# Nineteen slots for the experts' weights, a float32 gather one pair ahead, a down projection in column halves, and padded addresses

## The chip, the cores and the metric

The kernel runs on one core of a Trainium2 chip. A core has a matrix engine (TensorE, PE in the profile, with its weight loads as PEld), VectorE (DVE), ScalarE (ACT), GpSimd (POOL) and SyncE (SP), which here issues the transfers, and 16 DMA engines. The metric is the device time of one execution in microseconds; lower is better. The kernel before takes 2124.92 us, the median of three runs (2123.91 to 2125.03 us).

## The reference

Two transformer blocks over 256 tokens of 1024 features, in float32. The first is a hybrid layer: sparse attention, a gated recurrence and retention, merged through branch and output projections, and then a hierarchical mixture of experts. The second has four feed-forward layers, a spatial gating unit and stick-breaking attention. The change lies around the experts:

```python
gates = (jax.nn.one_hot(g_sel, N_GROUPS, dtype=jnp.float32)[:, :, None] * w_group[:, None, :]).astype(x.dtype)
...
for gi in range(N_GROUPS):
    hg = jax.nn.silu(jnp.einsum('nd,edf->nef', x, wg[gi])) * jnp.einsum('nd,edf->nef', x, wu[gi])
    y = y + jnp.einsum('nef,efd->nd', hg * gates[:, gi, :, None], wd[gi])
```

There are 4 groups of 8 experts, of width 512; a token takes one group and two of its experts, so that most of the gates are zero.

## The kernel before

Almost all matmuls outside the experts work on weights that come in units of 1 MB. `stage` (L214) loads a unit into one of three `ws` buffers. `load_split` rounds half of it to float32r on ScalarE (`wh`, L247) and subtracts on VectorE (`wl`, L248), and `mm3` (L268 to L270) multiplies weights and data, each in two parts, in three float32r matmuls. `wh` and `wl` have rings of three buffers in the pool `stg`; in the second block a further pool, `whx`, gives three more of each (`whx`, `wlx`), and the two rings are used in turn, three and three.

The experts (`experts`, L1121) go by pairs, 16 of them. A pair takes 12 units of 1 MB: for each of its two experts two for gate, two for up and two for down, 192 units in all. They lie in 13 slots: seven `b8` buffers (`we`), three `wx`, three `ws`. `route` fills all slots ahead (L1182). `both` consumes two slots, one for each expert of the pair, whose outputs stand in the two halves of the partitions, and then issues two further loads, which SyncE starts when the slot's last reader is done. A float32 matmul shows as two records in the profile, so a call of `both` is 16 records.

Up to 64 tokens (`CAP`) of an expert are gathered by a matmul with one-hot places. `places` makes them on VectorE for four experts at once (128x512). `gather` multiplies the normalized rows, in two float32r parts `hi` and `lo`, with the places, 256 columns for a chunk `k` of 128 features; each `k` has a PSUM bank of its own, and ScalarE copies it out with gain and shift (L1158, 128x256). A quad of experts is gathered one quad ahead, in halves, one in each pair.

`pair` (L1198) runs gate and up (four calls of `both`), silu on ScalarE (L1208), the product on VectorE (L1209), the previous pair's `spread`, four transposes of the product (L1214) with their copy (`actT`, L1216), the transposes of the places (L1221), the gates (L1223), `gsl` on VectorE (L1227), `ot` on ScalarE (L1228), the gather ahead (L1156), down (two calls of `both`, each over half of the inputs and all 1024 columns in two banks), and `dh` (L1237) and `dl` (L1238), the result in two float32r parts. `spread` (L1246, L1247) adds them to the tokens' rows with eight matmuls. After pair 0, a branch (`overflow`) handles experts with more than 64 tokens, and is not taken with these inputs.

The order on each engine is set when the program is built, by a scheduler with simulated times (`schedule_with_timeline_sim=True`), except where a chain or a `no_sync` fixes it.

Of the kernel before, what the change touches and what calls it, by code (L numbers as in the profile page):

```python
# [34 lines left out]
NE_B8, NE_MIX = 7, 3  # L35
ADA_EVERY, ADA_FROM = 3, 6
FRONT = 4
TCK = dict(schedule_with_timeline_sim=True)
# [80 lines left out]
def pack(inp):  # L119
# [39 lines left out]
    ed = g("expert_w_down")[0].reshape(NE, 2, 2, 128, 1024).transpose(0, 1, 3, 2, 4).reshape(NE, 2, 128, 2048)  # L159
# [21 lines left out]
class Program:  # L181
# [45 lines left out]
    def load_split(self, ap, kt, n=2048):  # L227
# [227 lines left out]
    def run(self):  # L455
        tc, nc, d = self.tc, self.nc, self.d
        with ExitStack() as es:
            self.main = es.enter_context(tc.tile_pool(name="main", bufs=1))
            self.small = es.enter_context(tc.tile_pool(name="small", bufs=1))
            self.stg = es.enter_context(tc.tile_pool(name="stg", bufs=3))  # L460
# [17 lines left out]
            self.hi = main.tile([128, KT, S], F32R, name="hi")  # L478
            self.lo = main.tile([128, KT, S], F32R, name="lo")
# [3 lines left out]
            eights = ExitStack()  # L483
            self.b8p = eights.enter_context(tc.tile_pool(name="b8", bufs=1))
# [4 lines left out]
            eights.close()  # L489
            self.whx = es.enter_context(tc.tile_pool(name="whx", bufs=1))  # L490
            self.ffn(0, fg)
# [14 lines left out]
            self.last_norm(g)  # L506

# [146 lines left out]
    def ada_row(self, chunk, o):  # L654
# [4 lines left out]
        r = self.small.tile([KT, 128], F32, name="adar", bufs=1)  # L659
# [50 lines left out]
    def hybrid(self):  # L710
# [89 lines left out]
        ocs = self.retention(at, cv, oc)  # L800
        self.branch(36, ocs, 8, mg, False, nk=4)
# [319 lines left out]
    def experts(self):  # L1121
# [3 lines left out]
        km, C = self.km, self.cap_limit  # L1125
        iota = km[:, 192:320]
        with tc.tile_pool(name="exw", bufs=1) as exw:
            xgs = [self.b8([128, KT, 4, CAP], name="xg") for _ in range(2)]
            self.slots = ([self.b8([128, 2048], name="we") for _ in range(NE_B8)]
                          + [exw.tile([128, 2048], F32, name="wx", bufs=NE_MIX) for _ in range(NE_MIX)]  # L1130
                          + [self.stg.tile([128, 2048], F32, name="ws", bufs=WS) for _ in range(WS)])
            self.units = [(2 * p + j, u) for p in range(NE // 2) for u in range(6) for j in range(2)]
            self.nload = self.nuse = 0
            with tc.tile_pool(name="moer", bufs=1) as self.moer:
                rank, topi, gates = self.route(km)
            with tc.tile_pool(name="moew", bufs=1) as self.moew:
                yp = self.acc4()
                ohs = {}

                def places(q):  # L1140

                    e4 = slice(4 * q, 4 * q + 4)
                    ohs[q] = oh = self.moew.tile([128, 2, 4, CAP], F32R, name="oh", bufs=2)
                    V.tensor_tensor(oh, iota[:, None, None, :CAP].to_broadcast([128, 2, 4, CAP]),
                                    rank[:, :, e4, None].to_broadcast([128, 2, 4, CAP]), op=OP.is_equal)
                    if C < CAP:
                        V.memset(oh[..., C:].bitcast(F32), 0.0)

                def gather(q, ks):

                    oh, xg = ohs[q], xgs[q % 2]
                    parts = [(hz, t) for hz in (self.hl, self.hh) for t in range(2)]
                    for k in ks:
                        ps = self.mms()[:, :4 * CAP].rearrange("p (a c) -> p a c", a=4)
                        for i, (hz, t) in enumerate(parts):
                            nc.tensor.matmul(ps, hz[:, t, k * 128:k * 128 + 128], oh[:, t], start=(i == 0), stop=(i == 3))  # L1156
# [3 lines left out]
                places(0)  # L1160
                gate, rgs = gates()
                gather(0, range(KT))
                pend = None
                for p in range(NE // 2):
                    q, ks = p // 2 + 1, range(4 * (p % 2), 4 * (p % 2) + 4)

                    def ahead():
                        if 4 * q < NE:
                            if p % 2 == 0:
                                places(q)  # L1170
                            gather(q, ks)

                    pend = self.pair(p, xgs[p // 2 % 2], ohs[p // 2], gate, yp, pend, ahead)
                    if p == 0:
                        self.overflow(topi, rgs, iota)
                self.spread(*pend)
                self.residual(yp, self.gt2)

    def load_slot(self):

        if self.nload < len(self.units):
            self.nc.sync.dma_start(self.slots[self.nload % len(self.slots)], self.d["w_e"][self.units[self.nload]])  # L1182
            self.nload += 1

    def both(self, outs, xs, ks, w, order):


        ws = [self.slots[(self.nuse + j) % len(self.slots)] for j in range(2)]
# [9 lines left out]
    def pair(self, p, xg, oh, gate, yp, pend, ahead):  # L1198
        nc, moe, V = self.nc, self.moew, self.nc.vector
        j0, e0, order = 2 * p % 4, 2 * p, []  # L1200
        ps = []
        for z in range(2):
            ps.append(self.mms())
            for u in range(2):
                self.both([(ps[z], 0)], lambda k: [xg[:, k, j0 + j] for j in range(2)], range(4 * u, 4 * u + 4),
                          lambda w, k, c: w[:, k % 4 * 512:k % 4 * 512 + 512], (order, KT - 1))
        a = moe.tile([128, 512], F32, name="act")
# [7 lines left out]
        at = moe.tile([128, 4, 2, CAP], F32, name="actT")  # L1215
# [3 lines left out]
        o2 = [oh[:, t, j0:j0 + 2].rearrange("p a c -> p (a c)").bitcast(F32) for t in range(2)]  # L1219
# [4 lines left out]
        ot = moe.tile([128, S], F32R, name="ot", bufs=2)  # L1224
        gs = moe.tile([128, 1], F32, name="gsl", bufs=2)
# [23 lines left out]
    def route(self, km):  # L1249

        nc, d, moer, small = self.nc, self.d, self.moer, self.small
        V, edge = nc.vector, self.edge
        before, iota = km[:, :128], km[:, 192:320]
        for _ in self.slots:
# [6 lines left out]
        ones = moer.tile([128, 128], F32R, name="ones_r")  # L1261
        nc.gpsimd.tensor_copy(ones, self.ones)
        earlier = moer.tile([128, 128], F32R, name="before_r")
# [4 lines left out]
        junk = moer.tile([128, 512], F32, name="rjunk")  # L1268
        xT = moer.tile([128, 2, KT, 128], F32, name="xT")
        ss, rs, lg = sm(2, "ssr"), small.tile([128, 2], F32, name="rsr"), sm(36, "lg")  # L1270
        hh = self.hh = self.hi.rearrange("p (a k) t -> p a (k t)", a=2)
        hl = self.hl = self.lo.rearrange("p (a k) t -> p a (k t)", a=2)
# [40 lines left out]
        self.chain(edge[1], nc.scalar.activation(hh[:, 0], self.x[:, 0], AF.Copy, scale=rs[:, 0:1]))  # L1313
        self.chain(edge[0], V.scalar_tensor_tensor(hl[:, 0], self.x[:, 0], rs[:, 0:1], hh[:, 0].bitcast(F32), op0=OP.mult, op1=OP.subtract))
# [6 lines left out]
        self.chain(edge[1], nc.scalar.activation(hh[:, 1], self.x[:, 1], AF.Copy, scale=rs[:, 1:2]))  # L1321
# [23 lines left out]
        found = V.tensor_mul(sel.rearrange("p a (g e) -> p a g e", g=4), og4, ssel[:, :, None, :].to_broadcast([128, 2, 4, 8]))  # L1345
        self.no_sync(V.scalar_tensor_tensor(hl[:, 1], self.x[:, 1], rs[:, 1:2], hh[:, 1].bitcast(F32), op0=OP.mult, op1=OP.subtract), found)
# [38 lines left out]
    def overflow(self, topi, rgs, iota):  # L1385

        nc, d, tc, moe = self.nc, self.d, self.tc, self.moew
# [429 lines left out]
```

## Time and profile before

| What | Value |
|---|---|
| median of three runs | 2124.92 us (2123.91 to 2125.03) |
| the profiled execution | 2124.35 us |
| its span | 2122.5 us |
| TensorE busy | 2044.1 us, 96% of the span |
| VectorE busy | 1111.3 us, 52% |
| ScalarE busy | 842.3 us, 40% |
| mean granted clock of TensorE | 0.993 |
| transfers | 503.17 MB, mean 237 GB/s |

The time of an execution is its span and some time around it. A share of busy time is a mean over the whole program; the expert stage lies at about 641 to 1117 us, the second block behind it. TensorE's records overlap, so that a row's duration is longer than the distance to the next row. A name such as `mm<-wh,hi` gives the output and the two operands.

### The profile page before, as it was taken

Reading aid. Unit: us, or ns where it says so; the run is one execution under the profiler, and the core shown is the slowest. Engines: PE = TensorE matmul, PEld = TensorE weight load, DVE = VectorE, ACT = ScalarE, POOL = GpSimd, SP = SyncE. Lnnn points to the kernel's source line nnn. Section 1 sums busy time; section 2 is a strip of 40 time slices with the busy share of each in tenths; the row PEclk is TensorE's granted clock in tenths of the full one; section 3 lists DMA queues with packets and bytes.
Section 4 is the critical chain, followed back from the end, with each engine's and each line's share of the span. In section 5 each row is a group of like instructions: output and inputs, shape, how many; then the busy total and the mean of one; then the engine's idle time right before and its main releaser. Section 6 shows DMA issues by size and latency. Waiting matters only on the chain.

```text
span 2122.5 us, 29320 instructions
## 1 busy us (share of the span) xinstructions
PE 2044.1 (96%) x12228; PEld 1608.6 (76%) x12228; DVE 1111.3 (52%) x1596; ACT 842.3 (40%) x1200; POOL 26.9 (1%) x40
## 2 busy tenths in 40 slices
PE   7999999999997999989989999999999999999998
PEld 5889889777773444333338998878999999989997
DVE  5886876755551111000017556656555755685555
ACT  4454334344442111111116445545444644475443
POOL 0000000000000000000000000000000000000000
PEclk9999999999998999999999999999999999999999
DMA  8655546455476999999995555544555455434552
GB/s 330 233 192 205 180 157 219 169 220 186 166 300 256 422 421 421 421 421 421 421 400 194 193 187 210 209 153 166 181 196 183 176 178 185 173 120 147 191 184 94
DMA packets 72124, 503.17 MB, mean 237 GB/s; under 512 B 8218, under 2 KB 10034, under 8 KB 11698
## 3 DMA queue, kind: packets, MB, share of 16 engines
q1 hardware_dynamic: 71986, 501.24, 62.1%
q8 instruction: 98, 1.61, 0.3%
q14 instruction: 40, 0.33, 0.0%
HBM read 500.14 MB, written 1.07 MB: 236 GB/s over the span
## 4 chain that ended last, share of the span: by engine, by line
PE 52%; DMA 12%; DVE 2%; issue 1%; ACT 0%; POOLq 0%; DVEq 0%; POOL 0%; SPq 0%; ACTq 0%
PE mm L268 10%; PE mm L270 10%; PE mm L269 10%; DMA we<-in_w_e 7%; PE mm L1193 6%; PE bg L268 5%; PE bg L270 5%; PE bg L269 5%; DMA ws<-in_w_e 3%; DMA wx<-in_w_e 3%; PE mm L411 1%; PE mm L1156 1%; DVE wl L248 0%; ACT wh L247 0%; DVE sn L1740 0%
## 5 line engine op out<-in xcount | busy, mean ns | idle before, releaser
L248 DVE TENSOR_TENSOR wl<-ws,wh 128x1024 fp32r<-128x1024 f32 x341 | 415.2, 1221 | 340.0 <-ACT wh L247 339.0
L247 ACT CAST wh<-ws 128x1024 fp32r<-128x1024 f32 x341 | 356.0, 1047 | 476.1 <-PE mm L270 386.3
L268 PE MATMUL mm<-hi,wl 128*128 128x256 f32 x1112 | 314.7, 283 | 2.7 <-DVE wl L248 2.6
L269 PE MATMUL mm<-lo,wh 128*128 128x256 f32 x1112 | 312.7, 281 | 0.1
L270 PE MATMUL mm<-hi,wh 128*128 128x256 f32 x1112 | 311.9, 280 | 0.0
L248 DVE TENSOR_TENSOR wlx<-ws,whx 128x1024 fp32r<-128x1024 f32 x165 | 201.1, 1222 | 141.5 <-ACT whx L247 141.2
L247 ACT CAST whx<-ws 128x1024 fp32r<-128x1024 f32 x165 | 172.3, 1049 | 174.5 <-PE mm L270 98.8
L268 PEld LDWEIGHTS mm<-hi,wl 128*128 128x128 f32 x1112 | 209.4, 188 | 6.4 <-DVE wl L248 3.9
L269 PEld LDWEIGHTS mm<-lo,wh 128*128 128x128 f32 x1112 | 209.5, 188 | 2.1 <-DVE lo L602 0.7
L270 PEld LDWEIGHTS mm<-hi,wh 128*128 128x128 f32 x1112 | 209.4, 188 | 0.7 <-issue 0.6
L269 PE MATMUL mm<-wl,hi 128*128 128x512 f32 (+1 forms) x468 | 179.9, 385 | 0.0
L268 PE MATMUL mm<-hi,wlx 128*128 128x256 f32 x640 | 179.0, 280 | 0.5 <-ACT rrow L1535 0.5
L270 PE MATMUL mm<-hi,whx 128*128 128x256 f32 x640 | 178.9, 279 | 0.0
L269 PE MATMUL mm<-lo,whx 128*128 128x256 f32 x640 | 178.7, 279 | 0.0
L270 PE MATMUL mm<-wh,hi 128*128 128x512 f32 (+1 forms) x468 | 177.5, 380 | 0.0
L268 PE MATMUL mm<-wh,lo 128*128 128x512 f32 (+1 forms) x468 | 173.9, 387 | 1.1 <-DVE lo L425 1.1
L1193 PE MATMUL mm<-we,xg 128*64 128x512 f32 x608 | 161.4, 599 | 4.7 <-DMA we<-in_w_e 4.7
L1209 DVE TENSOR_TENSOR act<-act,mm 128x512 f32<-128x512 f32 x16 | 11.0, 687 | 270.7 <-PE mm L1193 270.7
L268 PEld LDWEIGHTS mm<-hi,wlx 128*128 128x128 f32 x640 | 120.4, 188 | 1.8 <-ACT rrow L1535 0.8
L1193 PEld LDWEIGHTS mm<-we,xg 128*64 128x64 f32 x608 | 50.0, 138 | 94.6 <-issue 83.2
L269 PEld LDWEIGHTS mm<-lo,whx 128*128 128x128 f32 x640 | 120.5, 188 | 0.7
L270 PEld LDWEIGHTS mm<-hi,whx 128*128 128x128 f32 x640 | 120.5, 188 | 0.0
(490 smaller groups left out, 3432.6 us busy)
## 6 DMA issues: line engine op xcount, KB each, us to landing
we<-in_w_e SPq DMA_DIRECT2D x105, 1024.0 KB, 19.8
ws<-in_w_fi SPq DMA_DIRECT2D x88, 1024.0 KB, 4.8
wx<-in_w_e SPq DMA_DIRECT2D x45, 1024.0 KB, 19.8
ws<-in_w_fo SPq DMA_DIRECT2D x44, 1024.0 KB, 4.7
ws<-in_w_e SPq DMA_DIRECT2D x42, 1024.0 KB, 19.8
ws<-in_w_a SPq DMA_DIRECT2D x40, 1024.0 KB, 4.8
ws<-in_w_b SPq DMA_DIRECT2D x26, 1024.0 KB, 4.7
adw<-in_ada SPq DMA_DIRECT2D x17, 1024.0 KB, 7.2
```

The source lines that it names most:

```text
L247: w1 = nc.scalar.copy(wh[:, :m], src)
L248: w2 = nc.vector.tensor_sub(wl[:, :m], src, wh[:, :m].bitcast(F32))
L268: first = mm(out, ll, rh, start=start, stop=False)
L269: mm(out, lh, rl, start=False, stop=False)
L270: self.last_mm = mm(out, lh, rh, start=False, stop=stop)
L411: ins = nc.tensor.transpose(pss[k % 2][:, (k // 2) * 128:(k // 2) * 128 + 128], self.x[:, t, k * 128:k * 128 + 128], self.ident)
L1156: nc.tensor.matmul(ps, hz[:, t, k * 128:k * 128 + 128], oh[:, t], start=(i == 0), stop=(i == 3))
L1193: ins = self.nc.tensor.matmul(ps[j * 64:j * 64 + 64], xs(k)[j], w(ws[j], k, c), start=(k == 0), stop=(k == order[1]))
L1209: V.tensor_mul(a, a, ps[1])
```

## The change

- The slots: 19 in place of 13. `wp`, a tile of a new pool `exs`; `wr`, the place of `lo`; eight `b8` buffers; four `wx`; three `ws`; and two `whl` buffers. For the last, `wh` and `wl` become one tile `whl` of two halves, with two buffers, and a third of its own (`whd`), which in the experts holds first `xT` and then `dh` and `dl`. The first slot's load is issued in the hybrid layer, behind the last matmul of retention.
- The gather: float32 rows `xn` in one part, so that `lo` and the two VectorE subtractions that make it (L1314, L1346) are gone. Per pair 16 float32 matmuls of 128 columns, places of 128x256 for a pair, always one pair ahead (in pairs 0 to 14; before in 0 to 13). Four chunks `k` share a PSUM bank, and each of them has its own copy on ScalarE (128x128), in program order between the chunks' matmuls.
- The down projection: the weights are packed so that a unit holds half of the columns for all inputs. One call of `both` makes one half, and its `dh` and `dl` come before the other half's matmuls in program order.
- The addresses: unused tiles of 320, 128, 128 and 224 bytes a partition (`PADS`) in the pools `small`, `exs`, `whx` and `sgu`, and a longer `sn` in stick-breaking attention, move what lies behind them. `dynamic_dma_scratch_size=1024` is given to the compiler.
- `gsl`, `adar`, `act`, `ot` and the buffers of `overflow` change places; `overflow` follows the new packing.

The core of the diff:

```diff
-NE_B8, NE_MIX = 7, 3
+NE_B8, NE_MIX, NSLOT = 8, 4, 19
+PADS = 320, 128, 128, 224
...
-    ed = g("expert_w_down")[0].reshape(NE, 2, 2, 128, 1024).transpose(0, 1, 3, 2, 4).reshape(NE, 2, 128, 2048)
+    ed = g("expert_w_down")[0].reshape(NE, 4, 128, 2, 512).transpose(0, 3, 2, 1, 4).reshape(NE, 2, 128, 2048)
...
+    def pad(self, pool, n, name):
+
+        pool.tile([128, n // 4], F32, name=name)
+
...
+    def whl(self, shape, dt, last):
+        return self.stg.tile(shape, dt, name="whd", bufs=1) if last else self.stg.tile(shape, dt, name="whl", bufs=WHL - 1)
+
...
-            j = self.nhalf % (WHL + WH2)
+            j = self.nhalf % (WHL + WH2 if self.whx else WHL)
...
-                wh = self.stg.tile([128, 1024], F32R, name="wh", bufs=WHL)
-                wl = self.stg.tile([128, 1024], F32R, name="wl", bufs=WHL)
+                whl = self.whl([128, 2, 1024], F32R, j == WHL - 1)
+                wh, wl = whl[:, 0], whl[:, 1]
...
+            self.pad(self.small, PADS[0], "pad0")
...
+            self.exs = eights.enter_context(tc.tile_pool(name="exs", bufs=1))
+            self.slots = [self.exs.tile([128, 2048], F32, name="wp")]
...
+            self.pad(self.exs, PADS[1], "pad1")
...
+            self.pad(self.whx, PADS[2], "pad2")
...
+        self.no_sync(self.load_slot(), self.last_mm)
         self.branch(36, ocs, 8, mg, False, nk=4)
...
+        self.xn, spare = [self.main.tile([128, 2, 1024], F32, name=n, tag="hl", bufs=2) for n in ("xnr", "wr")]
+        with tc.tile_pool(name="exw", bufs=1) as self.exw:
+            self.slots.append(spare.rearrange("p a c -> p (a c)"))
+            self.slots += [self.b8([128, 2048], name="we") for _ in range(NE_B8)]
+            xgs = self.b8([128, 2, KT, 2, CAP], name="xg")
+            self.slots += [self.exw.tile([128, 2048], F32, name="wx", bufs=NE_MIX) for _ in range(NE_MIX)]
+            self.slots += [self.stg.tile([128, 2048], F32, name="ws", bufs=WS) for _ in range(WS)]
+            self.slots += [self.whl([128, 2048], F32, False) for _ in range(WHL - 1)]
+            rank, topi, gates = self.route(km)
+            self.dhl = self.whl([128, 2, 2, 512], F32R, True)
...
+            def gather(p):
+
+                oh, xg = ohs[p], xgs[:, p % 2]
+                for k0 in range(0, KT, 4):
+                    ps = self.mms().rearrange("p (k a c) -> p k a c", k=4, a=2)
+                    for k in range(k0, k0 + 4):
+                        for t in range(2):
+                            nc.tensor.matmul(ps[:, k - k0], self.xn[:, t, k * 128:k * 128 + 128], oh[:, t], start=(t == 0), stop=(t == 1))
                         gain, shift = self.a2c[:, k:k + 1], self.sh2c[:, k:k + 1]
-                        nc.scalar.activation(xg[:, k], ps, AF.Identity, bias=shift, scale=gain)
...
+                        nc.scalar.activation(xg[:, k], ps[:, k - k0], AF.Identity, bias=shift, scale=gain)
...
+                if p + 1 < NE // 2:
+                    places(p + 1)
+                    gather(p + 1)
...
-        pd = self.mms(2)
-        for u in range(2):
-            self.both([(pd[h], h * 512) for h in range(2)], lambda k: [at[:, k, j] for j in range(2)], range(2 * u, 2 * u + 2),
-                      lambda w, k, c: w[:, k % 2 * 1024 + c:k % 2 * 1024 + c + 512], (order, 3))
-        dh = self.stg.tile([128, 2, 512], F32R, name="dh", tag="wh", bufs=WHL)
-        dl = self.stg.tile([128, 2, 512], F32R, name="dl", tag="wl", bufs=WHL)
+        dh, dl = self.dhl[:, 0], self.dhl[:, 1]
         for h in range(2):
-            nc.scalar.activation(dh[:, h], pd[h], AF.Copy, scale=gs)
-            V.scalar_tensor_tensor(dl[:, h], pd[h], gs, dh[:, h].bitcast(F32), op0=OP.mult, op1=OP.subtract)
+            pd = self.mms()
+            self.both([(pd, 0)], lambda k: [at[:, k, j] for j in range(2)], range(4),
+                      lambda w, k, c: w[:, k * 512:k * 512 + 512], (order, 3))
+            nc.scalar.activation(dh[:, h], pd, AF.Copy, scale=gs)
+            V.scalar_tensor_tensor(dl[:, h], pd, gs, dh[:, h].bitcast(F32), op0=OP.mult, op1=OP.subtract)
...
-        for _ in self.slots:
+        while self.nload < NSLOT:
             self.load_slot()
...
-        xT = moer.tile([128, 2, KT, 128], F32, name="xT")
+        xT = self.whl([128, 2, KT, 128], F32, True)
...
-        self.chain(edge[1], nc.scalar.activation(hh[:, 0], self.x[:, 0], AF.Copy, scale=rs[:, 0:1]))
-        self.chain(edge[0], V.scalar_tensor_tensor(hl[:, 0], self.x[:, 0], rs[:, 0:1], hh[:, 0].bitcast(F32), op0=OP.mult, op1=OP.subtract))
+        self.chain(edge[1], nc.scalar.activation(self.xn[:, 0], self.x[:, 0], AF.Copy, scale=rs[:, 0:1]))
...
+        self.pad(sp, PADS[3], "pad3")
...
-                sn = sp.tile([128, 4 * S + 8], F32, name="sn", bufs=2)
+                sn = sp.tile([128, 4 * S + 64], F32, name="sn", bufs=2)
```

## Rows read from the trace of the kernel before

**Rows 1.** Windows: stretch, length, engines' busy time, clock, DMA share, GB/s.

```profile
635.00:650.00 15.00, 10.19 (x56) 7.47 (x57) 6.38 (x33) 5.16 (x11) 1.01 (x2) 0.77 0.01 2
...
700.00:836.00 136.00, 132.60 (x642) 55.73 (x641) 13.84 (x27) 22.69 (x43) 0.00 (x0) 1.00 1.01 421
836.00:1096.00 260.00, 239.52 (x1129) 98.36 (x1127) 23.63 (x46) 40.44 (x76) 0.00 (x0) 1.00 1.01 421
```

**Rows 2.** Timeline of SyncE's DMA issues: start, length, line, buffer and source, count.

```profile
616.44 5.91 SPq L1182 DMA_DIRECT2D ws<-in_w_e  x2
...
649.91 10.63 SPq L1182 DMA_DIRECT2D we<-in_w_e  x7
...
686.51 3.78 SPq L1182 DMA_DIRECT2D we<-in_w_e  x3
```

**Rows 3.** Chain of waits, expert stage's first half: start, length, engine, line, count.

```profile
680.06 16.32 PE mm L1193 x64
...
696.47 0.70 DVE act L1209
...
700.43 20.75 PE mm L1193 x96
...
750.13 0.70 DVE act L1209
...
752.09 2.00 PE mm L1156 x16
...
833.73 0.70 DVE act L1209
```

**Rows 4.** Chain of waits, the expert stage's second half and its end.

```profile
836.54 19.82 DMA we<-in_w_e
...
1096.46 3.66 PE mm L1193 x14
1100.21 0.70 DVE act L1209
...
1109.24 0.69 ACT dh L1237
...
1112.78 1.13 DVE wl L248
...
1116.62 0.92 PE mm L411 x3
```

**Rows 5.** Timeline of TensorE in the first block: float32 matmuls of 128 columns.

```profile
333.49 0.39 PE L1041 MATMUL bg<-bi,att 128*128 128x128 f32 x2
...
335.05 0.39 PE L1042 MATMUL bg<-bi,att 128*128 128x128 f32 x2
```

**Rows 6.** Waits from 575 to 1110 us: waiter, releaser, total us, times, longest.

```profile
PE mm L1193 <- PEq L1395: 5.9, 1, 5.9
ACT ot L1228 <- DVE gsl L1227: 5.4, 16, 0.4
```

**Rows 7.** Groups by form on ScalarE: count, busy us, mean ns, idle before.

```profile
L424 ACT ACTIVATE hi<-mm,cc 128x128 fp32r<-128x128 f32 x80 | 25.7, 365 | 35.6 <-PE mm L411 29.0 <-DVE lo L425 6.5
```

**Rows 8.** Groups by form on TensorE from 1130 to 2122 us.

```profile
L269 PE MATMUL mm<-lo,wh 128*128 128x256 f32 x688 | 192.7, 280 | 0.0
...
L269 PE MATMUL mm<-lo,whx 128*128 128x256 f32 x640 | 178.7, 279 | 0.0
L268 PE MATMUL bg<-whx,fl 128*128 128x512 f32 x188 | 73.9, 393 | 0.6 <-DVE fl L333 0.6
L269 PE MATMUL bg<-wlx,fh 128*128 128x512 f32 x188 | 73.5, 391 | 0.0
...
L268 PE MATMUL bg<-wh,fl 128*128 128x512 f32 x164 | 65.4, 399 | 0.2 <-DVE fl L333 0.2
...
L269 PE MATMUL bg<-wl,fh 128*128 128x512 f32 x164 | 64.8, 395 | 0.0
```

**Rows 9.** Groups by form on TensorE from 0 to 640 us.

```profile
L270 PE MATMUL mm<-wh,och 128*128 128x512 f32 x64 | 25.3, 395 | 0.0
```

More of the change, by code (lines that the diff above doesn't have):

```diff
@@ L483, in run @@
             eights = ExitStack()
+            self.exs = eights.enter_context(tc.tile_pool(name="exs", bufs=1))
+            self.slots = [self.exs.tile([128, 2048], F32, name="wp")]
+            self.units = [(2 * p + j, u) for p in range(NE // 2) for u in range(6) for j in range(2)]
+            self.nload = self.nuse = 0
+            self.pad(self.exs, PADS[1], "pad1")
             self.b8p = eights.enter_context(tc.tile_pool(name="b8", bufs=1))
@@ L506, in run, with parts @@
             self.last_norm(g)
+    def parts(self):
+        self.hi, self.lo = [self.main.tile([128, KT, S], F32R, name=n, tag="hl", bufs=2) for n in ("hi", "lo")]
     def last_norm(self, g):
@@ L1124, in experts @@
         nc, tc, d, V = self.nc, self.tc, self.d, self.nc.vector
-        km, C = self.km, self.cap_limit
+        km, C, exs = self.km, self.cap_limit, self.exs
         iota = km[:, 192:320]
[L1127 to L1156, printed above, removed]
-                        gain, shift = self.a2c[:, k:k + 1], self.sh2c[:, k:k + 1]
-                        nc.scalar.activation(xg[:, k], ps, AF.Identity, bias=shift, scale=gain)
[L1160 to L1177, printed above, removed]
@@ new lines, in experts, with places, ahead @@
+        self.xn, spare = [self.main.tile([128, 2, 1024], F32, name=n, tag="hl", bufs=2) for n in ("xnr", "wr")]
[8 more added lines that the diff above has]
+            self.dhl = self.whl([128, 2, 2, 512], F32R, True)
+            yp = self.acc4()
+            ohs = {}
+            def places(p):
+                e2 = slice(2 * p, 2 * p + 2)
+                ohs[p] = oh = exs.tile([128, 2, 2, CAP], F32, name="oh", bufs=2)
+                V.tensor_tensor(oh, iota[:, None, None, :CAP].to_broadcast([128, 2, 2, CAP]),
+                                rank[:, :, e2, None].to_broadcast([128, 2, 2, CAP]), op=OP.is_equal)
+                if C < CAP:
+                    V.memset(oh[..., C:], 0.0)
+            def gather(p):
[5 more added lines that the diff above has]
+                            nc.tensor.matmul(ps[:, k - k0], self.xn[:, t, k * 128:k * 128 + 128], oh[:, t], start=(t == 0), stop=(t == 1))
+                        gain, shift = self.a2c[:, k:k + 1], self.sh2c[:, k:k + 1]
+                        nc.scalar.activation(xg[:, k], ps[:, k - k0], AF.Identity, bias=shift, scale=gain)
+            places(0)
+            gate, rgs = gates()
+            gather(0)
+            pend = None
+            for p in range(NE // 2):
+                def ahead():
+                    if p + 1 < NE // 2:
+                        places(p + 1)
+                        gather(p + 1)
+                pend = self.pair(p, xgs[:, p % 2], ohs[p], gate, yp, pend, ahead)
+                if p == 0:
+                    self.overflow(topi, rgs, iota)
+            self.spread(*pend)
+            self.residual(yp, self.gt2)
@@ L1179, in load_slot @@
     def load_slot(self):
         if self.nload < len(self.units):
-            self.nc.sync.dma_start(self.slots[self.nload % len(self.slots)], self.d["w_e"][self.units[self.nload]])
+            ins = self.nc.sync.dma_start(self.slots[self.nload % NSLOT], self.d["w_e"][self.units[self.nload]])
             self.nload += 1
+            return ins
     def both(self, outs, xs, ks, w, order):
-        ws = [self.slots[(self.nuse + j) % len(self.slots)] for j in range(2)]
+        ws = [self.slots[(self.nuse + j) % NSLOT] for j in range(2)]
@@ L1198, in pair @@
     def pair(self, p, xg, oh, gate, yp, pend, ahead):
-        nc, moe, V = self.nc, self.moew, self.nc.vector
-        j0, e0, order = 2 * p % 4, 2 * p, []
+        nc, exs, V = self.nc, self.exs, self.nc.vector
+        e0, order = 2 * p, []
         ps = []
@@ L1204, in pair @@
             for u in range(2):
-                self.both([(ps[z], 0)], lambda k: [xg[:, k, j0 + j] for j in range(2)], range(4 * u, 4 * u + 4),
+                self.both([(ps[z], 0)], lambda k: [xg[:, k, j] for j in range(2)], range(4 * u, 4 * u + 4),
                           lambda w, k, c: w[:, k % 4 * 512:k % 4 * 512 + 512], (order, KT - 1))
-        a = moe.tile([128, 512], F32, name="act")
+        a = exs.tile([128, 512], F32, name="act")
         nc.scalar.activation(a, ps[0], AF.Silu)
@@ L1214, in pair @@
             nc.tensor.transpose(pt[:, ft * 128:ft * 128 + 128], a[:, ft * 128:ft * 128 + 128], self.ident)
-        at = moe.tile([128, 4, 2, CAP], F32, name="actT")
+        at = exs.tile([128, 4, 2, CAP], F32, name="actT")
         nc.scalar.copy(at.rearrange("p a b c -> p (a b c)"), pt)
         po = self.mms()
-        o2 = [oh[:, t, j0:j0 + 2].rearrange("p a c -> p (a c)").bitcast(F32) for t in range(2)]
+        o2 = [oh[:, t].rearrange("p a c -> p (a c)") for t in range(2)]
         for t in range(2):
@@ L1258, in sm @@
             return small.tile([128, 2, n], F32, name=name)
-        ones = moer.tile([128, 128], F32R, name="ones_r")
+        ones = self.exs.tile([128, 128], F32R, name="ones_r")
         nc.gpsimd.tensor_copy(ones, self.ones)
-        earlier = moer.tile([128, 128], F32R, name="before_r")
+        earlier = self.exs.tile([128, 128], F32R, name="before_r")
         nc.gpsimd.tensor_copy(earlier, before)
@@ L1320, in route @@
         self.chain(edge[1], nc.scalar.activation(junk[:, :1], self.ones[:, :1], AF.Exp))
-        self.chain(edge[1], nc.scalar.activation(hh[:, 1], self.x[:, 1], AF.Copy, scale=rs[:, 1:2]))
+        self.chain(edge[1], nc.scalar.activation(self.xn[:, 1], self.x[:, 1], AF.Copy, scale=rs[:, 1:2]))
         self.res = self.rest = self.edge = None
@@ L1385, in overflow @@
     def overflow(self, topi, rgs, iota):
-        nc, d, tc, moe = self.nc, self.d, self.tc, self.moew
+        nc, d, tc, exs = self.nc, self.d, self.tc, self.exs
         C = self.cap_limit
@@ L1424, in overflow @@
                             ps = mm()[:, :128]
-                            parts = [(hz, t) for hz in (self.hh, self.hl) for t in range(2)]
-                            for i, (hz, t) in enumerate(parts):
-                                nc.tensor.matmul(ps, hz[:, t, k * 128:k * 128 + 128].bitcast(F32), oh[:, t],
-                                                 start=(i == 0), stop=(i == 3))
+                            for t in range(2):
+                                nc.tensor.matmul(ps, self.xn[:, t, k * 128:k * 128 + 128], oh[:, t], start=(t == 0), stop=(t == 1))
                             xg = ov.tile([128, 128], F32, name="oxg", bufs=2)
```

29 lines of the change are left out of this document (13 added, 16 removed).

## The prediction

> **What bounds the kernel now.** The profiled execution took 2124.35 us, of which 2122.5 us are the span and 1.85 us lie around it; the median of the three runs, 2124.92 us, is 0.57 us longer. I make the sum on the profiled time and carry the 0.57 us over at the end. A difference under 0.2% (4.2 us) is about what a measurement of this kernel can't tell from none.
>
> I read first the table by stage [rows 1]. TensorE is busy in 132.60 of 136 us between 700 and 836 us, but in only 239.52 of 260 us between 836 and 1096 us, at a full granted clock in both; the DMA engines are full in both (421 GB/s, share 1.01). So the expert stage is bound by TensorE first and by the weights' transfers later. Between 635 and 650 us, 2 GB/s move: all thirteen slots are full, and nothing frees one.
>
> Next SyncE's issues [rows 2]. The first thirteen units are all issued by about 622 us; the fourteenth goes out at 649.91 us, when pair 0 has used two slots, and pair 0's other units follow. They land, the queue runs dry, and the next unit goes out at about 686 us, since TensorE stands 5.9 us at the overflow branch [rows 6]. By 686 us thus 25 of 192 units have been issued.
>
> Then the chain of waits. In its first half [rows 3] it runs on TensorE: the product after silu (`L1209`) comes at 696.47, 750.13 and 833.73 us, which is 53.66 us for two pairs and then 83.60 us for three, 27.87 us each. The first two are shorter because in one of them (700.43, 96 matmul records without a break) the spread of the pair before was kept for the time in which TensorE waits for that product; the two unequal gaps give 53.66 − 27.87 = 25.79 us for that filled pair, 2.08 us less. From 836.54 us the chain goes over to the weights, in steps of 19.82 us [rows 4], thirteen in all, up to 1096.46 us. A step is a queue of eight units, so a unit takes 2.48 us and a pair 12 × 2.48 = 29.7 us. As a check, the 167 units left at 686 us need 414 us from there, to about 1100 us, and the last step of the chain lands at 1096.46 us. After that come the last pair's product at 1100.21 us, the last down matmul before 1109.24 us, 9.03 us later, and the second block's first transposes of new rows at 1116.62 us.
>
> **The change part by part.**
>
> *Six more slots.* Six more units move before 650 us; 6 × 2.48 = 15 us fits the idle stretch of 635 to 650 us [rows 1]. The transfers then end 14.9 us earlier, and a stage bound by them alone would end its down projection at 1109.24 − 14.9 = 1094.4 us. That is a floor, since TensorE must get there too.
>
> *Gather in float32.* Before, a pair has 16 gather records in 2.00 us [rows 3]. After, a pair has 16 float32 matmuls of 128 columns; these show as two records each, at 0.112 us a record in a loop of the first block (eight rows of two from 333.49 to 335.05 us, 0.22 us apart) [rows 5]. That is 32 × 0.112 = 3.57 us, or 1.57 us more a pair. It falls on TensorE, which is the bound in the pairs that the slots speed up. Pair 14 gets a gather that it did not have. The gather ahead of pair 0 has 16 matmuls in place of 32 and stays at about its length.
>
> *TensorE's end of the stage.* The product of pair 1 comes at 696.47 + 1.57 (the longer gather of pair 0) − 0.7 (one `dh` of 0.69 us [rows 4] of pair 0's is made earlier, ahead of the branch) = 697.4 us. Fourteen gaps between products follow, of 27.87 + 1.57 = 29.44 us unfilled, or 27.36 us where the spread fills the wait for the product, and then 9.03 us. None filled: 697.4 + 412.2 + 9.0 = 1118.6 us. One filled, as before: 1116.5 us. All filled: 1089.5 us, and then the transfers' 1094.4 us binds. The gain of the slots thus hangs on how many waits are filled. The order is set when the program is built, and the trace shows what it is now: filled where weights lie ready (the pair after 700.43 us), not filled in the later ones. More slots should fill more pairs; between one and fourteen I take five: 1108.2 us, which is −1.0 us against 1109.24 us. Bounds −14.9 and +9.4 us.
>
> *One bank for four chunks of the gather.* Four k chunks share a PSUM bank, and each is copied out by ScalarE on its own. ScalarE's `ot` waits 5.4 us in 16 times for VectorE's `gsl` [rows 6], though both only read, and different columns of one bank: accesses of two engines to a bank are kept in order. So the matmul of chunk k+1 waits for the copy of chunk k. One such round is four records (0.45 us) and their drain (0.39 − 0.22 = 0.17 us) [rows 5], the copy of 0.365 us [rows 7], and two hand-overs, estimated at 0.05 us each: about 1.1 us. If the two banks take turns, eight chunks take 4 × 1.1 = 4.4 us, 0.85 us over the 3.57 us above; if down matmuls stand in between, nothing. Bounds: 0 and 15 × 0.85 = 12.8 us; a worse order is a rival below. I take 0.1 us a gather, 1.5 us, because each pair has 32 down records ready beside it.
>
> The Trainium skill, page "Perfetto Trace Analysis", section "Optimizing Tensor Performance", asks that independent matmul groups rotate through different PSUM banks, so that one group's evacuation overlaps the next group's matmuls; the change turns from one bank for each chunk to four chunks in one. By that rule the waits are not hidden, and its rival below holds; the `ot` row is the only one here that bears on it, and it shows the ordering but at 0.34 us a time.
>
> *Start of the stage.* The two `lo` subtractions leave VectorE; `xT` takes a buffer that the last of `w_out` still holds. Nothing of it is longer than about 2 us; bounds −1 and +2, taken as 0. The six early loads go out on SyncE by about 630 us, as the last `w_out` halves free `whl`; queued behind them are only pair 0's loads, which wait until 649.91 us [rows 2] in any case. If they came late instead, the unit that they hold up costs 2.48 us each.
>
> *Down projection in halves.* Same records, so nothing on TensorE. At the very end, `dl` of the second half ends at 1112.78 us [rows 4], because both halves' `dh` and `dl` and a weight split stand between. With half 0 done under half 1, it ends 0.69 + 0.75 us after the last matmul, at about 1110.7 us: −2.1 us. The 1.13 us of `wl` behind it can also go before: −1.1 us. I take −3; bounds −1.2 and −3.7 us.
>
> *Padded addresses.* The same matmul runs at two paces, by the pool of its weights. In the feed-forward output, with `whx`, 393 and 391 ns; with `wh`, 399 and 395 ns (the third form is as the second) [rows 8]. The 128x256 form shows 279 ns from `whx` and 280 ns from `wh`. The first block uses `wh` alone and shows 395 ns in its 128x512 forms [rows 9], of which the branches and the output have 480. If `wh`, which the pads move, falls in with `whx`: 164 × (6 + 4 + 4) ns = 2.3 us, 480 × 4.5 ns = 2.2 us, and 1 ns on 3336 records of 128x256 with `wh`, 3.3 us: −7.8 us. If `whx` falls in with `wh` instead: 564 × 4.7 ns and 1920 × 1 ns, +4.5 us. No row shows what the pads do to either pool. As all pools are moved at once, and two of the three terms have a faster row beside them in the same stretch, I take −5.5 us.
>
> Sum: −1.0 + 1.5 + 0 − 3 − 5.5 = −8.0 us: 2116.4 us on the profiled time, 2117 us on the median.
>
> **The rivals.**
>
> 1. *The slots pay in full.* TensorE's waits are filled in at least twelve pairs, the down projection ends on the transfers at 1094.4 us, and with −3 and −5.5 us the time is 2124.9 − 23.4 = 2101.5 us, at least 2099 us. For it: DMA at 1.01 with TensorE at 0.92 of the late stretch. Against it: only one of the five gaps that TensorE sets is filled now.
>
> 2. *Slots don't fill the waits and pads do nothing.* End of down at 1116.5 us (+7.3), stall +1.5, tail −3: 2130.7 us; with half of the pads' price, 2128 us. TensorE then takes over from the transfers for the whole stage. For it: four unfilled gaps; against it: they are from pairs in which the weights came late.
>
> 3. *Slower, by the bank.* The gather's chunks wait for ScalarE, two banks in turn: 1116.5 + 12.8 us (+20.1), −3, −5.5: 2136.5 us. It decides from 0.63 us a gather on (the sum without its stall is −9.5 us, over fifteen gathers). If instead all eight chunks go one after the other, a gather takes 8.8 us, 5.2 us over, 78 us in all, and the time is about 2200 us.
>
> **How the numbers follow.** The likeliest case has three to eight filled pairs and pads of 0 to −7.8 us: 2108 to 2124 us, chance 0.45, of which 0.07 lie within 0.2%. Rival 1: 0.15, faster. Rival 2: 0.19, of which 0.10 within 0.2%, 0.08 slower, 0.01 faster. Rival 3 with banks in turn: 0.14, of which 0.13 slower; all in a row: 0.07. So faster 0.38 + 0.15 + 0.01 = 0.54, within 0.2% 0.18, slower 0.28. The range, 2100 to 2138 us, leaves out the chunks in a row, the lower edge of rival 1 and the upper of rival 3, about 0.18.
>
> **What the profile after would show.** The slots: 19 units issued before the first gather, 161 left at the second pair, and transfers that end 15 us earlier or have gaps of their own. TensorE: gaps between products of 27.4 to 29.4 us; spread records next to the wait for the product, or in the middle of the next pair. The bank: gather records with idle time released by ScalarE's copy, none if I am right. The tail: `dl` about 1.4 us after the last down matmul. The pads: 391 ns for `wh` and `whl` alike. The prediction is wrong if gaps exceed 30 us, if the pads leave the paces or worsen them, or if the stage's start grows by more than 2 us.

## The result, and the profile after

The changed kernel takes 2148.43 us (2147.75 to 2152.89, four runs), the kernel before 2124.53 us (2123.91 to 2125.03, four runs): a ratio of 1.0117, 95% interval 1.0100 to 1.0135. It is 24 us slower; 2117 us were forecast, 2100 to 2138 us as range. The profiled execution has a span of 2146.7 us, 24.2 us above that of before.

The windows of the changed kernel, against [rows 1]:

```profile
635.00:650.00 15.00, 14.07 (x68) 8.27 (x70) 2.30 (x14) 3.64 (x8) 0.74 (x2) 0.83 0.14 43
...
700.00:836.00 136.00, 132.46 (x650) 59.35 (x648) 13.21 (x26) 28.84 (x59) 0.00 (x0) 1.00 1.00 413
836.00:1096.00 260.00, 253.11 (x1222) 108.87 (x1220) 23.42 (x48) 50.39 (x107) 0.00 (x0) 1.00 0.99 405
```

TensorE is now busy in 253.11 of 260 us of the late stretch, where it was in 239.52 us, and the DMA engines move 405 in place of 421 GB/s: the transfers are no longer the bound. That half of the forecast came true. But TensorE, with hardly an idle moment, needs longer for the same work. SyncE's issues, against [rows 2], show the nineteen slots filled as planned; the last of them goes out at 625.61 us:

```profile
625.61 0.38 SPq L1199 DMA_DIRECT2D we<-in_w_e  x1
...
646.92 0.33 SPq L1199 DMA_DIRECT2D wp<-in_w_e  x1
```

The chain of waits of the changed kernel, one gap between two products, against [rows 3]:

```profile
941.84 0.44 PE mm L1211
...
942.38 0.70 DVE act L1227
...
943.12 0.65 PE mm L1232 x4
...
944.34 1.00 PE mm L1175 x8
945.33 3.58 PE mm L1211 x16
948.92 1.09 PE mm L1175 x8
950.01 1.00 PE mm L1211 x2
951.01 1.09 PE mm L1175 x8
...
953.03 3.58 PE mm L1211 x14
956.61 1.09 PE mm L1175 x8
957.70 1.00 PE mm L1211 x2
958.70 0.43 PE bg L1262
...
959.82 13.89 PE mm L1211 x62
...
973.81 0.70 DVE act L1227
```

Read the lines `L1175` (gather) and `L1211` (down, then gate and up) together. Before, an unfilled gap held one gather of 16 records in one piece, and the `L1193` records stood (in most) in two pieces, of 34 and 62 records, with the spread between them. Now the gather comes in four pieces of 8 records, and the down, gate and up records in five: 16, 2, 14, 2, 62. The two pieces of 2 records take 1.00 us each, where 2 records in a long piece take 0.43 us. The gap is 31.43 us, as in seven of the fourteen; in six earlier ones (pieces of 26, 10, 4, 4 and 52) it is 30.60 us, and in one 30.23 us. In all of them TensorE stands still for the product: here from the end of the last record, 942.28 us, to the first transpose (`L1232`) at 943.12 us, 0.84 us. No spread fills that time. From the product at 695.88 us to the last at 1129.77 us the fourteen gaps sum to 433.9 us. The last `dh` starts at 1139.09 us, against 1109.24 us [rows 4], and the second block's first transposes 4.35 us later; before it was 6.14 us (1109.24 to 1115.38 us on TensorE's timeline). The timeline of that end:

```profile
1139.09 0.69 ACT L1253 ACTIVATE whd<-mm,gsl 128x512 fp32r<-128x512 f32 x1 [1.81 <-PE mm L1211]
...
1139.81 0.75 DVE L1254 SCALAR_TENSOR_TENSOR whd<-mm,gsl,whd 128x512 fp32r<-128x512 f32 x1 [1.28 <-ACT whd L1253]
...
1140.74 1.23 DVE L256 TENSOR_TENSOR whl<-ws,whl 128x1024 fp32r<-128x1024 f32 x1 [0.18 <-ACT whl L255]
...
1143.44 0.63 PE L419 MATMUL mm<-k,x 128*128 128x128 f32 x4 [1.63 <-DVE x L1561]
```

Where the 24.2 us lie, from the same markers in both traces: the first block's last output matmul starts 4.7 us earlier (630.20 and 625.45 us); from there to the product of pair 1 it takes 4.2 us longer; the fourteen gaps take 30.2 us longer (403.7 and 433.9 us); the last product to the last `dh` 0.3 us longer; from there to the transposes 1.8 us less; the second block, from those transposes to its last matmul, 3.5 us less, and what stands behind that matmul 0.3 us less.

### The profile page after: what moved, and what is told of

It reads as the page before. It is cut to its first block, busy times and chain, and to the rows that moved or that the text cites. A ratio compares the mean times of both kernels' runs of the same rounds, so it can differ in the third digit from the quotient of the medians.

```text
span 2146.7 us, 29952 instructions
## 1 busy us (share of the span) xinstructions
PE 2083.3 (97%) x12484; PEld 1634.6 (76%) x12484; DVE 1110.4 (52%) x1602; ACT 866.2 (40%) x1264; POOL 24.7 (1%) x40
## 4 chain that ended last, share of the span: by engine, by line
PE 65%; DVE 2%; ACT 1%; issue 0%; DMA 0%; POOLq 0%; DVEq 0%; POOL 0%; ACTq 0%
PE mm L1211 16%; PE mm L276 10%; PE mm L278 10%; PE mm L277 10%; PE bg L276 5%; PE bg L277 5%; PE bg L278 5%; PE mm L1175 3%; PE bg L1262 1%; PE bg L1263 1%; PE mm L419 1%; DVE act L1227 0%; PE mm L1232 0%; PE mm L1780 0%; PE mm L1743 0%
## 5 line engine op out<-in xcount | busy, mean ns | idle before, releaser
L256 DVE TENSOR_TENSOR whl<-ws,whl 128x1024 fp32r<-128x1024 f32 x228 | 277.7, 1220 | 220.9 <-ACT whl L255 220.1
L255 ACT CAST whl<-ws 128x1024 fp32r<-128x1024 f32 x228 | 238.4, 1048 | 295.3 <-PE mm L278 250.1
L276 PE MATMUL mm<-hi,whl 128*128 128x256 f32 x836 | 235.4, 282 | 1.1 <-DVE whl L256 1.0
L277 PE MATMUL mm<-lo,whl 128*128 128x256 f32 x836 | 233.8, 280 | 0.1
L278 PE MATMUL mm<-hi,whl 128*128 128x256 f32 x836 | 233.3, 279 | 0.0
L256 DVE TENSOR_TENSOR whd<-ws,whd 128x1024 fp32r<-128x1024 f32 x113 | 137.7, 1219 | 112.0 <-ACT whd L255 111.2
L255 ACT CAST whd<-ws 128x1024 fp32r<-128x1024 f32 x113 | 118.2, 1046 | 172.7 <-PE mm L278 127.6
L276 PEld LDWEIGHTS mm<-hi,whl 128*128 128x128 f32 x836 | 157.2, 188 | 3.3 <-issue 1.2
L277 PEld LDWEIGHTS mm<-lo,whl 128*128 128x128 f32 x836 | 157.2, 188 | 1.5 <-DVE lo L620 0.7
L278 PEld LDWEIGHTS mm<-hi,whl 128*128 128x128 f32 x836 | 157.2, 188 | 0.2
L277 PE MATMUL mm<-whl,hi 128*128 128x512 f32 (+1 forms) x304 | 118.0, 388 | 0.0
L278 PE MATMUL mm<-whl,hi 128*128 128x512 f32 (+1 forms) x304 | 116.3, 383 | 0.0
L276 PE MATMUL mm<-whl,lo 128*128 128x512 f32 (+1 forms) x304 | 114.8, 391 | 1.2 <-DVE lo L433 1.2
```

What stands on the lines that cost most here:

```text
L255: w1 = nc.scalar.copy(wh[:, :m], src)
L256: w2 = nc.vector.tensor_sub(wl[:, :m], src, wh[:, :m].bitcast(F32))
L276: first = mm(out, ll, rh, start=start, stop=False)
L277: mm(out, lh, rl, start=False, stop=False)
L278: self.last_mm = mm(out, lh, rh, start=False, stop=stop)
```

## The experiments

Each kernel was timed in rounds against the kernel before; the ratios are against that, with their 95% interval.

**The copies behind the bank's matmuls.** The copies of a bank's four chunks leave the loop over the chunks:

```diff
                         for t in range(2):
                             nc.tensor.matmul(ps[:, k - k0], self.xn[:, t, k * 128:k * 128 + 128], oh[:, t], start=(t == 0), stop=(t == 1))
+                    for k in range(k0, k0 + 4):
                         gain, shift = self.a2c[:, k:k + 1], self.sh2c[:, k:k + 1]
```

> The changed kernel, but with the four copies of a bank on ScalarE behind all eight of the bank's gather matmuls, so that no gather matmul waits for a copy; built so, all 16 gather matmuls of a pair stand together on TensorE, and the spread stands behind the last up matmul in the first four gaps and near the start of gate and up in the others. Theory A (cuts): in the changed kernel the gather and the spread cut the stream of down, gate and up matmuls, which run two at a time in two halves of the array, into five pieces a pair instead of two, each cut costs about 0.4 us and a matmul left alone by a cut 0.4 us more. Then a gap between products falls from 30.6 to 31.4 us to about 27.4 us where the spread stands late and 29.5 to 30 us elsewhere, and the time from 2148.4 us to about 2122 us. Theory B (the float32 gather by itself is the cost): gaps stay at 30.6 to 31.4 us and the time at 2148 us.

Measured: 2124.82 us, ratio 0.9996 (0.9986 to 1.0005), 23.6 us less than the changed kernel by one line moved. The gaps are 26.5 us once and 27.47 us three times, then 32.0 us once and 29.9 us. Theory A holds, theory B falls: the gather's 32 float32 records are all still there. In the later gaps the spread still stands in the middle, in two halves with seven matmuls (14 records) between them.

**The spread kept for the wait.** In addition, the spread of the pair before may not start before the last up matmul, from the third pair on:

```diff
+            self.spread(*pend, self.last_both if p > 1 else None)
...
+                if after is not None:
+                    self.no_sync(ins, after)
```

> As the kernel with the copies last, and the spread of the pair before is also kept behind the last up matmul in every pair from the third on, where TensorE waits for the product. Theory A: gaps of 27.4 us until the weights' transfers bind (29.8 us a pair), the last down matmul ends near 1095 us instead of 1139 us, and the time is about 2104 us, below both kernels. Theory B: only the wait for the product is filled, 2.1 us a gap, and the time is about 2119 us.

Measured: 2104.55 us, ratio 0.9904 (0.9888 to 0.9921): faster than both kernels, and within 1 us of theory A. Its chain of waits shows the whole gap (`L1212` is `both`, `L1264` the spread, `L1234` the transposes):

```profile
697.61 3.68 PE mm L1175 x32
701.28 20.75 PE mm L1212 x96
722.03 0.43 PE bg L1264
...
724.08 0.44 PE mm L1234 x4
```

The gather stands in one piece (3.68 us), the 96 records run in one, and the spread takes the place of the wait. After a first gap of 26.53 us the gaps are 27.47 us up to the product at 996.9 us, then 29.0, 29.8 and 29.8 us: there the transfers bind. Its windows, with TensorE busy all the time until 836 us and 420 GB/s throughout:

```profile
700.00:836.00 136.00, 136.00 (x720) 63.70 (x719) 14.64 (x30) 29.22 (x64) 0.00 (x0) 1.00 1.01 420
836.00:1096.00 260.00, 256.74 (x1339) 120.67 (x1338) 26.58 (x54) 55.51 (x120) 0.00 (x0) 1.00 1.01 420
```

**Thirteen slots, in the changed kernel and in this one.** `NSLOT` is 13, nothing else changes.

```diff
-NE_B8, NE_MIX, NSLOT = 8, 4, 19
+NE_B8, NE_MIX, NSLOT = 8, 4, 13
```

> The changed kernel with 13 slots used instead of 19, all else the same. Theory A: with gaps of 30.6 to 31.4 us against 29.8 us for a pair's transfers, TensorE is the bound in every pair, and six slots fewer change nothing: within 0.2% of 2148.4 us. Rival (the slots pay, and something else costs more than the loss shows): up to 14.9 us slower, 2163 us.

> The kernel with the copies last and the spread late, with 13 slots in place of 19. Theory (with gaps of 27.5 us the transfers bind, at 2.48 us a unit): the end of the down projection comes 6 x 2.48 = 14.9 us later, and the time rises from 2104.6 to about 2119 us. Rival (the slots buy nothing here either): 2105 us.

Measured: 2147.75 us, ratio 1.0107 (1.0090 to 1.0124), for the changed kernel with 13 slots: nothing lost against 2148.43 us. With the copies last and the spread late, 13 slots give 2121.24 us, ratio 0.9979 (0.9970 to 0.9989): 16.7 us more than with 19, where 14.9 us were worked out. After a first of 26.53 us its gaps are 27.47 us up to 832.6 us, then 29.4 to 29.8 us, and once 31.4 us. So the six slots are worth what the transfers' pace says, but only in a kernel whose TensorE can follow.

**Cuts alone.** On the kernel with the spread late, TensorE's order is forced by a chain, and the copies stay behind their bank's matmuls: four gather matmuls, 8 down, 4 gather, 1 down, 4 gather, 7 down, 4 gather, and then gate and up; and the same with 8, 2 and 6 down matmuls.

```diff
+                    self.count += 1
+                    if self.count in (8, 9, 16):
+                        next(self.groups, None)
...
-                    if self.count in (8, 9, 16):
+                    if self.count in (8, 10, 16):
```

> The kernel with the copies last and the spread late, with TensorE's order forced: the gather ahead is cut into four groups of four matmuls, with 8, 1 and 7 matmuls of the down projection between them and the last group ahead of the next gate, as in most pairs of the changed kernel. No gather matmul waits for a copy here. Theory A (a cut costs, and a lone matmul costs more): three more cuts of 0.39 us and two lone matmuls of 0.41 us, so that a gap rises from 27.47 to about 29.5 us and the time from 2104.6 to about 2123 us. Rival (the cost in the changed kernel came from the wait for ScalarE's copies): gaps stay at 27.5 us and the time at about 2105 us.

> As the kernel with cuts after 8, 9 and 16 down matmuls, but with cuts after 8, 10 and 16, so that no matmul of one expert stands without that of the other beside it. Theory A: three cuts of 0.39 us and no lone matmul, a gap of about 28.6 us and about 2112 us. Rival (only the number of cuts counts): 29.5 us and 2123 us, as with the odd cuts.

Measured: 2123.33 us, ratio 0.9990 (0.9980 to 0.9999), with gaps of 29.35 us, for the odd cuts; 2111.03 us, ratio 0.9932 (0.9915 to 0.9948), with gaps of 28.51 us, for the even ones: theory A holds in both. The chains (`L1217` is `both`), of the odd cuts first:

```profile
733.96 1.09 PE mm L1175 x8
735.05 1.00 PE mm L1217 x2
736.05 1.09 PE mm L1175 x8
737.14 3.58 PE mm L1217 x14
```

and of the even cuts:

```profile
731.68 1.09 PE mm L1175 x8
732.77 1.01 PE mm L1217 x4
733.78 1.09 PE mm L1175 x8
734.87 2.73 PE mm L1217 x12
```

A piece of 4 records takes 1.01 us, and a piece of 2 records, half of the work, 1.00 us. Three cuts cost 28.51 − 27.47 = 1.04 us, 0.35 us each; the two matmuls left alone cost 29.35 − 28.51 = 0.84 us, 0.42 us each. In these gaps the chain runs on TensorE alone, without a copy in it, so that the cuts by themselves explain what the changed kernel lost: its gap of 31.43 us is 27.47 + 1.88 (odd cuts) + 2.08 us (the spread not in the wait, 27.87 − 25.79 from [rows 3]). Counted piece by piece, both kinds of gap have four cuts more than the gap of 27.47 us and the unfilled 0.84 us; the pieces of 16, 2, 14, 2 and 62 records leave four matmuls alone, those of 26, 10, 4, 4 and 52 two. At 0.35 and 0.42 us each that makes 31.39 and 30.55 us, where 31.43 and 30.60 us were measured.

**Waits alone.** On the kernel with the spread late, each copy stands between its bank's matmuls again, and the first down matmul may not come before the last gather matmul.

```diff
-                    for k in range(k0, k0 + 4):
                         gain, shift = self.a2c[:, k:k + 1], self.sh2c[:, k:k + 1]
...
+        for ins in self.gmm if p else ():
+            self.no_sync(order[32], ins)
```

> The kernel with the spread late, and each chunk's copy again between the matmuls of its bank as in the changed kernel, but no down matmul may stand between the gather's matmuls. It prices the wait for ScalarE's copy alone: by the round of 1.1 us that the prediction worked out, a gather of 3.68 us takes 4.4 us if the two banks take turns (gaps of 28.2 us, about 2109 us) and 8.8 us if the chunks go one after the other (gaps of 32.6 us, about 2165 us).

Measured: 2114.31 us, ratio 0.9949 (0.9933 to 0.9966), with gaps of 28.72 us. Its chain of waits in the gather (`L1176` the matmuls, `L1178` the copies):

```profile
727.85 0.37 ACT xg L1178
728.22 0.04 issue
728.27 0.73 PE mm L1176 x4
728.99 0.02 issue
729.02 0.47 ACT xg L1178
729.48 0.04 issue
729.53 0.73 PE mm L1176 x4
```

The two banks take turns, as one bound of the prediction had it: the next matmul starts 0.04 us after the copy. The wait costs 28.72 − 27.47 = 1.25 us a gather, where 0.85 us were worked out, since the copy takes 0.47 us and the round 1.26 us (728.27 to 729.53 us). The cuts with which the order hid this wait cost more in seven gaps of the changed kernel (1.88 us) and less in six (30.60 − 27.47 − 2.08 = 1.05 us). Over the fourteen gaps the two prices are close: here the gaps sum to 401.1 us, which with 2.08 us a gap for the spread would be 430.2 us, an estimate, against 433.9 us.

**The spread late in the kernel before.** The edit that keeps the spread for the wait, alone, on the kernel before.

> The kernel before, with only the spread kept behind the last up matmul from the third pair on. Theory (with 13 slots the weights' transfers set the end of the stage): the gaps that TensorE sets fall from 27.9 to 25.8 us, the chain goes over to the transfers some pairs earlier, the last down matmul still ends near 1109 us, and the time stays within 0.2% of before. Rival (TensorE's cuts set it there too): four gaps of 2.1 us, 8 us faster, 2117 us.

Measured: 2125.53 us, ratio 1.0002 (0.9992 to 1.0011): no change, as its theory had it, though early gaps fall to 25.79 us, the very number that the prediction took from two unequal gaps. VectorE's timeline of that kernel:

```profile
748.29 0.69 DVE L1210 TENSOR_TENSOR act<-act,mm 128x512 f32<-128x512 f32 x1 [12.33 <-PE mm L1193]
...
774.08 0.69 DVE L1210 TENSOR_TENSOR act<-act,mm 128x512 f32<-128x512 f32 x1 [12.33 <-PE mm L1193]
```

From 801.6 us on its gaps are 29.8 to 30.0 us, but for one of 31.1 us, and its chain of waits goes over to the weights at 778.00 us, where before it did at 836.54 us [rows 4]:

```profile
778.00 19.82 DMA we<-in_w_e
```

With thirteen slots the transfers set the end, whatever TensorE gains.

**The pads.** All four tiles and the longer `sn` are taken out of the changed kernel; then the first tile alone is left in.

```diff
-PADS = 320, 128, 128, 224
+PADS = 0, 0, 0, 0
...
-PADS = 320, 128, 128, 224
+PADS = 320, 0, 0, 0
```

> The changed kernel without the four unused tiles and with the old size of sn. Theory (the addresses set the pace): the first block, 4.7 us shorter than before up to its last output matmul, and the second block, 3.9 us shorter, lose this again, and the time rises by about 8.6 us to 2157 us. Rival (the gain comes from other edits, as wh and wl in one tile): no change, 2148 us.

> The changed kernel with the first unused tile alone (320 bytes in the pool small), the other three gone and sn at its old size. The kernel without any pad took 2167.7 us, with all of them 2148.4 us. Theory (the first pad moves the staging pool and all pools behind it): nearly all of it comes back, 2148 to 2152 us, with the 128x256 forms at 279 to 280 ns again. Rival (each pool needs its own): the forms with whx stay at 282 ns, and the time is about 2156 us or more.

Measured: 2167.66 us, ratio 1.0197 (1.0180 to 1.0214), without pads, 19.2 us more than with them; 2160.17 us, ratio 1.0165 (1.0148 to 1.0182), with the first alone. The same matmul in three kernels, groups by form in the second block; first the changed kernel:

```profile
L277 PE MATMUL mm<-lo,whl 128*128 128x256 f32 x544 | 151.7, 279 | 0.0
...
L277 PE MATMUL mm<-lo,whx 128*128 128x256 f32 x640 | 179.3, 280 | 0.0
```

without pads:

```profile
L278 PE MATMUL mm<-lo,whl 128*128 128x256 f32 x544 | 153.3, 282 | 0.0
...
L278 PE MATMUL mm<-lo,whx 128*128 128x256 f32 x640 | 180.5, 282 | 0.0
```

and with the first pad alone:

```profile
L278 PE MATMUL mm<-lo,whl 128*128 128x256 f32 x544 | 152.0, 279 | 0.0
...
L278 PE MATMUL mm<-lo,whx 128*128 128x256 f32 x640 | 180.4, 282 | 0.0
```

The first pad gives `whl` its 279 ns back, and `whx` stays at 282 ns: the theory of one pad for all falls, and its rival holds. Which of the other three tiles, or the longer `sn`, makes up the rest of the 19.2 us was not run one by one. The weights' place is not all, either. A form of the first block, in the changed kernel and then with the first pad alone:

```profile
L278 PE MATMUL mm<-whl,och 128*128 128x512 f32 x44 | 17.1, 389 | 0.0
...
L279 PE MATMUL mm<-whl,och 128*128 128x512 f32 x44 | 17.4, 394 | 0.0
```

`whl` lies behind the first pad alone and has the same place in both; `och` is a `b8` buffer, behind the second pad too. So the place of the data counts as well.

The expectation for the kernel without pads had the direction, and its rival falls; it missed the size, 8.6 us against 19.2 us. It took the pads against the kernel before; but without pads the changed kernel is slower than before in both blocks. The first block's last output matmul starts at 633.30 us (before 630.20 us, with pads 625.45 us), and the second block, from its first transposes to its last matmul, takes 1008.7 us (before 998.9 us, with pads 995.4 us). That the new tiles did this by moving the buffers is likely, since the pads take it back, but which of them did was not run.

## Why the prediction was wrong

**What bounds the kernel, and the floor:** right. The transfers' end of 1094.4 us and the filled gap of 27.36 us were worked out from the trace before; the kernel with the spread late shows 27.47 us and then the transfers' 29.8 us, and the 14.9 us of six slots were measured as 16.7 us.

**The float32 gather:** right as a sum of records. It was put at 3.57 us and takes 3.68 us in one piece.

**How many waits are filled:** this step failed, and with it the likeliest case. Five of fourteen were taken; none was filled. More slots did not move the spread. The order that was built put it into the middle of the records, and in two pieces, as the halves' `dh` and `dl` come one after the other: 5 × 2.08 = 10.4 us too little. The argument, that the spread waits for the product where weights lie ready, was read from one pair. With the copies behind the bank's matmuls the same build fills the first four gaps by itself, so that the place of the gather's copies decided this too.

**One bank for four chunks:** this is the step that failed most. The prediction saw the wait for the copy, bounded it by 12.8 us over fifteen gathers, and took 1.5 us, "because each pair has 32 down records ready beside it". The order did fill the wait with them, and it was the filling that cost: the fourteen gaps sum to 433.9 us, where 412.2 us were worked out for unfilled gaps, 21.7 us more. The bound "if down matmuls stand in between, nothing" was the false sentence. The other bound, 12.8 us, was too low as well: fifteen waits of 1.25 us make 18.8 us, an estimate from the run with waits alone. The trace of before could have told the price of a cut: its filled pair saved 2.08 us, of which the wait that it filled, 0.84 us (777.90 to 778.74 us in the pair below), is the lesser part; its 96 records take 20.75 us in one piece [rows 3], and in an unfilled pair 7.87 and 13.89 us in two, 1.01 us more:

```profile
754.09 7.87 PE mm L1193 x34
...
764.01 13.89 PE mm L1193 x62
...
778.74 0.66 PE mm L1214 x4
```

The Trainium skill, page "Perfetto Trace Analysis", section "Optimizing Tensor Performance", has independent groups rotate through banks so that evacuation and the next group overlap. The runs agree that several groups in one bank with copies between them cost, 1.25 us a gather as waits and 23.6 us in all as they were ordered here. They don't ask for one bank a chunk: four chunks in one bank take 3.68 us, 0.1 us over their records, once the copies come behind all of them.

**Rival 3** named the place and the sign, but by ScalarE's wait and with 2136.5 us; what came is the filled wait, at 2148.4 us, between its two forms. It was outside the range.

**Start of the stage:** taken as 0, at most +2 us; from the last output matmul to the product of pair 1 it is 4.2 us longer. The sum had 0.9 us of it (1.57 − 0.7 us, under TensorE's end of the stage). Of the 4.2 us, 1.8 us come up to the product of pair 0 (660.32 − 630.20 us before, 657.34 − 625.45 us now) and 2.4 us from there to that of pair 1 (36.15 and 38.54 us). The gather of pair 0 is itself cut by gate matmuls now, and that of pair 1 in pair 0 by down matmuls; what these cuts have of either part was not measured.

**Tail:** −3 us taken, −1.8 us measured. `dl` ends 1.47 us after `dh` starts, as forecast, but a weight split of 1.23 us still stands between it and the residual (1140.74 us above).

**Pads:** −5.5 us taken, bounds −7.8 and +4.5; the two blocks together show −8.2 us, a little past the bound. The mechanism, a pool's place setting the pace of a form, is shown by the runs without pads and with one, though not by the weights' pool alone, as the prediction had it (`och` above). It also took the pads as a gain on the kernel before. They first had to make good what the changed kernel loses without them, 3.1 us in the first block and 9.8 us in the second, which no row of before could show. So the closeness of −8.2 to −5.5 us is in part luck.

**The sum:** −8.0 + 10.4 (no wait filled) + 20.2 (21.7 less the 1.5 us taken for the bank) + 3.3 (start) + 1.2 (tail) − 2.7 us (pads) is +24.4 us, against 24.2 us between the two spans.

What stays open: why the built order takes the cuts. That it does so where a matmul waits for a copy is shown (the order changes with the copies' place alone); what it weighs was not measured.

## What to carry to other kernels

A wait on TensorE that is filled with other matmuls is not free when those run two at a time in halves of the array: look at the number of pieces that a stream is in, and at pieces that split such a pair, before looking at idle time. Here neither filling the wait nor leaving it was cheap; moving the copies behind all matmuls of their bank took the wait itself away. A change that widens one resource (slots) is paid out only if the next bound, TensorE here, is brought down with it; price the two together. When tiles are added, compare the pace of unchanged matmuls by form, since their addresses moved too.

## What the runs showed of the hardware

Matmuls of 64 columns on the two halves of the array ran side by side: 96 records took 20.75 us, 0.43 us for two. A cut of such a stream by the gather's matmuls cost 0.35 us, and a matmul without its partner 0.42 us more. A matmul that waited for ScalarE's copy out of its bank started 0.04 us after the copy's end. The pace of a 128x256 matmul went from 279 to 282 ns with the place of its weights, and that of a 128x512 matmul from 389 to 394 ns with the place of its data; 800 unused bytes a partition and a longer `sn` decided 19.2 us of 2167.7 us.
